# A partial sum put back into the accumulator banks, rounded channel sums, and a shift by matmul, in a one-core decoder step on Trainium2

## The chip, the cores and the metric

The kernel runs on one core of one Trainium2 chip. The metric is the device time of one execution in microseconds (us). A kernel's time is the median of several executions.

## What is computed

One step of a hybrid decoder with two layers, over 1024 prompt tokens and 8 sampled tokens, with 2048 channels. The first layer is a pooling mixer with a SiLU gate, the second a sliding-window attention with a gate. Around each layer stands a normalization with a scaled residual. Cut to the matrix products and what the change touches:

```python
# layer A
z = x @ w_in;  u, gate = z[..., :D_POOL], z[..., D_POOL:]          # "ai"
d = multiscale_pool(u) - u;  d = einsum(d, w_grp) * scale
h = layer_norm(ALPHA * x + (d * silu(gate)) @ w_out, g, b)         # "ao"
kv = h @ w_kv
# layer B
z = h @ w_in;  q, gate = z[..., :D_ATTN], z[..., D_ATTN:]          # "bi" (with kv)
o = attn_core(rope(q), k, v, window=128, sinks)
y = layer_norm(ALPHA * h + (o * silu(gate)) @ w_out, g, b)         # "bo"

def layer_norm(x, g, b):
    mu = mean(x);  var = mean(square(x - mu))
    return (x - mu) * rsqrt(var + LN_EPS) * g + b
```

Everything is held with the channels on the 128 partitions and the tokens along the free dimension, so a mean over channels is a sum over partitions and over 16 tiles.

## The kernel before, in words

**Phases and products.** The four big projections are the phases ai, ao, bi and bo, with 16, 8, 18 and 8 positions; a position is a pair of 128-channel output tiles (m = 0 and 1). The tokens are two chunks: c = 0 with 512, and c = 1 with 520 (512 prompt tokens and the 8 sampled ones). Each position is a 2x2 block product in seven multiplications, idx 0 to 6, instead of eight. A phase does them in three groups: A (idx 0 and 5, one unit of 512 columns each), C (idx 1, 3 and 6) and B (idx 2 and 4). Units of C and B have two halves of 260 columns (HV), and a half is a tick of 24 matmuls; a unit of A makes two ticks of 12 matmuls. In the last four positions of bo B all units of the first half come before those of the second.

**Passes.** Every operand is split into a rounded part and a rest, both in the four-byte matmul format fp32r: a ScalarE cast makes the first (L384 for weights, L515 for activations) and a VectorE subtraction the second (L392, L521). Each product is three fp32r matmuls, high by high, high by low and low by high: L588, L589 and L590 in `run_unit`.

**Banks.** A ring of three PSUM banks (`psD`) holds what is being accumulated, one bank is for small sums (`psO`), and four are for attention or for the tail (`psW`). `post` empties a bank after its tick:
- idx 0: the negated product is stored to DRAM (`n0`; L612).
- idx 1 and 3: group C starts from the negated product of idx 0, which `seed` loads nine ticks ahead and ScalarE copies into the bank at two ticks and one tick ahead (L677). The partial sums after idx 1 and idx 3 go to z[:, 0] and z[:, 1], by ScalarE (L625) in ai and bi, and by VectorE with the scaled residual (L621) in ao and bo. At idx 3 z is stored to DRAM (`bb`) through GpSimd's queue.
- idx 5 and 6: the outputs of the first chunk (L632).
- idx 2 starts a fresh bank, and idx 4 goes on in it. VectorE empties it after idx 2 as z[:, 1] less the bank (L641), which is the output m = 1 of the second chunk, and after idx 4 as the bank with z[:, 0] (L643 in ao and bo, L645 in ai and bi), which is m = 0. `recall` loads z nine ticks ahead (L698).
- For the gate channels of ai, a ScalarE Silu (L739) runs over each finished pair of tiles of the second chunk, eight in all.

**Normalization.** A side generator (`ln_gen`) normalizes a chunk, some steps per tick. Its sums over channels are in `j_gen`: for each stretch two fp32 matmuls of the constant J, which fills every partition with the mean (L813). L884 to L901 are its elementwise steps; L887 is the scale and bias on ScalarE. The output of the first position pair is used to shift all others ahead of squaring: its mean is made by fp32 matmuls in `shifted` (L1097) and, for the second chunk of bo, in `tail_full` (L1156). For bo B from position 2 on, the shift is subtracted on VectorE from both halves of z (L701). `tail_sums` (L1231), `tail_stats` (L1243 to L1245) and `tail_norm2` (L1261) end the kernel with the last outputs; L1193 and L1197 square and add the last pieces. What is left of the generators when the units are through is stepped before `tail_end`.

**Attention in bi.** Scores (L1429) go to the four banks `pS`, are copied (L1491) and masked on VectorE (L1492); L1293 applies the rotation to a tile whose partner was fetched by copies from SBUF to SBUF; L1572 is the activation of the gate.

**The order.** Instructions go to each engine in the order in which the program writes them (`in_order`). A planner writes them: `on` and `at` put an action at a tick with a rank; `soft` gives it to an engine with a due tick and lets it go early when that engine's metered work is less than 1.5 us ahead of TensorE's; the side generators step when VectorE and ScalarE are calm, or every few ticks, if four whole slots of the 53 SBUF slots are free. `start` loads the constants (cst, which holds J, at L1747) and makes the first operands.

Of the kernel before, what the change touches and what calls it, by code (L numbers as in the profile page):

```python
# [16 lines left out]
P = 128  # L17
# [139 lines left out]
class Kern:  # L157
    def __init__(self, ctx, tc, io):
# [17 lines left out]
        self.sgd = [one.tile([P, 8, NDEC], F32, name=f"sgd{i}") for i in range(2)]  # L176
        self.mem = Mem(pool("mem", bufs=1), NSLOT)
# [388 lines left out]
    def run_unit(self, u):  # L566
# [7 lines left out]
        for n, cs in enumerate(hs):  # L574
            w = cs.stop - cs.start
            key = ph, pos, cs.start
            if idx in (0, 2):
                self.bank[key] = self.psD()
            new = idx in (0, 2)
            ps = self.bank[key]  # L580
            for n2 in range(8):
# [12 lines left out]
                if u.grp == "A" and n2 == 3:  # L594
                    self.end()
            if n == len(hs) - 1:
                self.w_done(u)
# [3 lines left out]
    def post(self, u, cs):  # L601
# [13 lines left out]
        elif idx in (1, 3):  # L615
# [4 lines left out]
            if ph in RES:  # L620
                nc.vector.scalar_tensor_tensor(  # L621
                    z, z, ALPHA, ps[:, :w], op0=ALU.mult, op1=ALU.add if i else ALU.subtract
                )
            else:
                nc.scalar.copy(z, ps[:, :w])  # L625
            if idx == 3 and fin:
                nc.gpsimd.dma_start(self.bb[ph][:, pos], s.v(2, TMAX))
                self.bs.pop((ph, pos)).free(True)
# [7 lines left out]
        else:  # L636
            z = self.bs[ph, pos].v(2, TMAX)
            m = 1 if idx == 2 else 0
            out = self.dest(ph, pos, m, 1)(cs)
            if m:  # L640
                nc.vector.tensor_sub(out, z[:, 1, cs], ps[:, :w])  # L641
            elif ph in RES:
                nc.vector.tensor_add(out, ps[:, :w], z[:, 0, cs])  # L643
            else:
                nc.vector.tensor_sub(out, ps[:, :w], z[:, 0, cs])  # L645
            if m == 0:
# [6 lines left out]
    def prepare(self):  # L653

        for u in self.units:
# [4 lines left out]
            elif u.idx == 2 and u is self.firstu(u):  # L660
                self.recall(u)

    def firstu(self, u):
        return u if self.tick[u.ph, u.pos, u.idx] == u.t else None
# [26 lines left out]
    def recall(self, u):  # L691
        ph, pos, t = u.ph, u.pos, u.t
        nc = self.nc
        s = {}

        def load():
            b = self.bs[ph, pos] = self.mem.full()
            nc.sync.dma_start(b.v(2, TMAX), self.bb[ph][:, pos])  # L698
        def shift():
            z = self.bs[ph, pos].v(2, TMAX)  # L700
            nc.vector.tensor_sub(z, z, self.sh[:, None, :].to_broadcast([P, 2, TMAX]))  # L701

        self.on(t - 9, load, 5)
        if ph == "bo" and pos > 1:
            self.on(max(t - 7, self.first["bo", "B"] + 7), lambda: self.soft("v", self.i, t - 2, shift))
# [21 lines left out]
    def done(self, ph, pos, m, c, cs=None):  # L727
        k = ph, pos // 2, m, c
        if ph == "ai":
# [6 lines left out]
            elif i % 2:  # L736
                s = self.box.pop(k)
                if c == 1:
# [67 lines left out]
    def j_gen(self, T, src, out):  # L806

        J = self.cst[:, K_J : K_J + P]
        for s in [slice(0, T)] if T <= 512 else HV:
            yield from self.quiet()  # L810
            ps = self.psO()[:, : s.stop - s.start]
            for i, a in enumerate(src):
# [1155 lines left out]
```

## Time and profile before

| what | us |
|---|---|
| median of 3 executions | 2356.5 |
| lowest and highest | 2353.34, 2358.8 |
| the profiled execution | 2353.2 |
| its span | 2351.4 |
| mean granted TensorE clock, share of full | 0.991 |
| ScalarE's casts of weights L384, 366 | 380.2 |
| VectorE's subtractions L392, 366 | 444.7 |
| waits of TensorE on other engines, the sum of its table of waits | 33.1 |

The stages in the profiled execution, in us from the start of the span: ai A from 7.9, C from 211.5, B from 510.2; ao A from 741.6, C from 832.3, B from 970.3; bi A from 1065.9, C from 1313.4, B from 1667.9; bo A from 1955.6, C from 2073.3, B from 2211.6 to 2327.4; the tail to 2351.4.

In a row of waits "PE pD L588 <- DVE m L641: 10.9, 5, 6.1" TensorE (PE) waited at line 588 for VectorE (DVE) at line 641, 10.9 us in all, five times, 6.1 at the longest. In a row of groups stand the line, engine, operation, tiles and shape, the count, the busy time in us, the mean of one in ns, and the idle time of the engine just before them with what ended it. In a row of windows stand the stretch, its length, the busy time and number of instructions of PE, PE's weight loads, DVE, ACT (ScalarE) and POOL (GpSimd), the granted clock, the share of the DMA engines and GB/s. A row of the timeline has the start, the duration, the engine and the line; what stands in brackets is the idle time ahead of it. Matmul records of a row stand in the order of issue; an fp32 matmul leaves two records.

### The profile page before, as it was taken

What the parts mean: (1) busy time and instruction counts of PE and PEld (TensorE: products, weight loads), DVE (VectorE), ACT (ScalarE), POOL (GpSimd) and SP (SyncE); (2) the same over time, 40 slices, a digit from 0 to 9 for tenths busy, and PEclk for the clock granted to TensorE, in tenths of its full rate; (3) what the DMA queues carried; (4) which work ended last, traced back from release to release, by engine and by line L of the source; (5) the groups of instructions that cost most, each with busy time, mean ns of one, the idle gap of its engine ahead of it and who ended that gap; (6) DMA issues with size and microseconds to landing.
All of it is one profiled execution on the core that took longest, in us unless ns stands there. A gap on an engine that the chain in (4) does not pass through costs nothing. (4 is left out here: it accounts for less than half of the span.)

```text
span 2351.4 us, 41872 instructions
## 1 busy us (share of the span) xinstructions
PE 2297.0 (98%) x16998; PEld 2134.2 (91%) x16998; DVE 1550.3 (66%) x1884; ACT 1029.2 (44%) x2071; POOL 208.1 (9%) x424
## 2 busy tenths in 40 slices
PE   8999999999999999999999999999999999999985
PEld 6888999999999799998777899999999997899985
DVE  6456746656676686686765855665666777687686
ACT  4344333333233432444655635454646565542334
POOL 1101101000101111000110110100000000111002
PEclk9999999999999999999999999999999999999998
DMA  9858666674749798896685766666645566898843
GB/s 388 302 181 285 221 224 234 210 255 130 265 140 333 236 349 280 283 315 234 229 301 167 271 223 215 220 210 221 195 140 150 172 197 210 267 383 273 283 143 118
DMA packets 194481, 555.63 MB, mean 236 GB/s; under 512 B 31088, under 2 KB 36080, under 8 KB 194288
## 3 DMA queue, kind: packets, MB, share of 16 engines
q1 hardware_dynamic: 152592, 402.42, 52.9%
q0 software_dynamic: 41696, 150.55, 16.4%
q8 instruction: 133, 2.18, 0.4%
q14 instruction: 60, 0.49, 0.1%
HBM read 372.04 MB, written 171.33 MB: 231 GB/s over the span
## 5 line engine op out<-in xcount | busy, mean ns | idle before, releaser
L588 PE MATMUL pD<-m,m 128*128 128x260 f32 (+1 forms) x4800 | 1463.1, 305 | 19.0 <-DVE m L641 10.9
L589 PE MATMUL pD<-m,m 128*128 128x260 f32 (+1 forms) x4800 | 1448.4, 302 | 0.9 <-DVE m L521 0.9
L590 PE MATMUL pD<-m,m 128*128 128x260 f32 (+1 forms) x4800 | 1448.0, 302 | 0.0
L588 PEld LDWEIGHTS pD<-m,m 128*128 128x128 f32 x4800 | 906.1, 189 | 72.5 <-issue 26.2
L589 PEld LDWEIGHTS pD<-m,m 128*128 128x128 f32 x4800 | 906.5, 189 | 37.4 <-DVE m L521 2.0
L590 PEld LDWEIGHTS pD<-m,m 128*128 128x128 f32 x4800 | 905.9, 189 | 35.9
L392 DVE TENSOR_TENSOR m<-m,m 128x1024 fp32r<-128x1024 f32 x366 | 444.7, 1219 | 181.4 <-ACT m L384 167.1
L384 ACT CAST m<-m 128x1024 fp32r<-128x1024 f32 x366 | 380.2, 1045 | 77.6 <-PE pD L589 15.2
L428 DVE TENSOR_TENSOR m<-m,m 128x1024 f32<-128x1024 f32 x200 | 243.8, 1219 | 20.2 <-PE pD L589 6.5
L632 ACT COPY m<-pD 128x260 f32<-128x260 f32 (+1 forms) x126 | 55.9, 444 | 325.2 <-PE pD L590 319.2
L625 ACT COPY m<-pD 128x260 f32<-128x260 f32 x136 | 51.1, 376 | 225.8 <-PE pD L590 225.6
L521 DVE TENSOR_TENSOR m<-m,m 128x1040 fp32r<-128x1040 f32 x112 | 135.2, 1235 | 16.9 <-ACT m L515 16.6
L515 ACT CAST m<-m 128x1040 fp32r<-128x1040 f32 x112 | 114.7, 1059 | 37.4 <-DMA m<-h 17.8
L1492 DVE TENSOR_TENSOR m<-pS,cst 128x1024 f32<-128x1024 f32 x32 | 39.1, 1222 | 93.8 <-ACT m L1491 93.7
L1465 ACT ACTIVATE m<-m,sm 128x128 f32<-128x128 f32 x256 | 99.2, 391 | 0.0
L641 DVE TENSOR_TENSOR m<-m,pD 128x260 f32<-128x260 f32 x100 | 42.2, 422 | 75.3 <-PE pD L590 75.2
L1030 PE MATMUL pD<-m,m 128*128 128x260 f32 (+1 forms) x576 | 91.5, 319 | 0.0
L1030 PEld LDWEIGHTS pD<-m,m 128*128 128x128 f32 x576 | 82.0, 188 | 8.3
L1478 ACT ACTIVATE m<-m,sm 128x128 f32<-128x128 f32 x256 | 81.8, 393 | 7.2 <-DVE sm L1473 7.1
L612 ACT ACTIVATE m<-pD 128x512 f32<-128x512 f32 x50 | 29.8, 596 | 124.2 <-PE pD L590 114.8
L1446 ACT COPY m<-pS 128x768 f32<-128x768 f32 (+1 forms) x32 | 29.1, 908 | 123.0 <-PE pS L1429 123.0
L645 DVE TENSOR_TENSOR m<-pD,m 128x260 f32<-128x260 f32 x68 | 29.0, 426 | 73.1 <-PE pD L590 72.9
(168 smaller groups left out, 1564.1 us busy)
## 6 DMA issues: line engine op xcount, KB each, us to landing
m<-in_wia SPq DMA_DIRECT2D x96, 512.0 KB, 5.4
m<-in_wib SPq DMA_DIRECT2D x96, 512.0 KB, 5.0
m<-in_woa SPq DMA_DIRECT2D x48, 512.0 KB, 5.7
m<-in_wob SPq DMA_DIRECT2D x48, 512.0 KB, 6.8
m<-in_x SPq DMA_DIRECT2D x36, 520.0 KB, 9.8
sbi<-m POOLq DMA_DIRECT2D x36, 512.0 KB, 4.2
m<-sbi SPq DMA_DIRECT2D x36, 512.0 KB, 4.5
sai<-m POOLq DMA_DIRECT2D x32, 512.0 KB, 5.0
```

What stands on the lines that cost most here:

```text
L384: self.nc.scalar.copy(e["hi"].r[:, :1024], e["raw"].a[:, :1024])
L392: self.nc.vector.tensor_sub(o.r[:, :1024], s.a[:, :1024], e["hi"].a[:, :1024])
L428: self.nc.vector.tensor_add(s[o].a[:, :1024], s[a].a[:, :1024], s[b].a[:, :1024])
L515: self.nc.scalar.copy(h.r[:, : 2 * TMAX], s.a[:, : 2 * TMAX])
L521: self.nc.vector.tensor_sub(o.r[:, : 2 * TMAX], s.a[:, : 2 * TMAX], h.a[:, : 2 * TMAX])
L588: nc.tensor.matmul(ps[:, :w], wh[:, s], h, start=new and n2 == 0, stop=False, skip_group_check=on)
L589: nc.tensor.matmul(ps[:, :w], wh[:, s], l, start=False, stop=False, skip_group_check=on)
L590: nc.tensor.matmul(ps[:, :w], wl[:, s], h, start=False, stop=n2 == 7, skip_group_check=on)
L632: self.evac(ph, pos)(self.dest(ph, pos, m, 0)(cs), ps[:, : cs.stop - cs.start])
L1030: nc.tensor.matmul(ps[:, : cs.stop - cs.start], ws[:, s], d[:, cs], start=f0 and k == 0, stop=l0 and k == 3,)
L1465: nc.scalar.activation(x["s3"][:, i, :], x["s3"][:, i, :], AF.Exp, bias=nm[:, i : i + 1], scale=0.125, accum_out=rs[:, i : i + 1],)
L1478: nc.scalar.activation(x["s3"][:, i, :], x["s3"][:, i, :], AF.Copy, scale=rs[:, i : i + 1])
```

## The change

- The second-chunk banks of idx 2 start from the partial sum: `recall` lets ScalarE copy z[:, 1], now stored negated, into the bank, at two ticks and one tick before its half. After idx 2 the bank is emptied by a ScalarE activation with scale -1, which also applies the Silu for the gate channels of m = 1, so four of the eight Silus of L739 go. After idx 4 VectorE adds z[:, 0], which a new VectorE operation (`both`) has combined from z[:, 0] and z[:, 1] in group C, up to four ticks after idx 3; the store to `bb` follows it.
- The channel sums are made of rounded parts: VectorE adds the two tiles of the pair, ScalarE rounds the sum, VectorE takes the rest, and two fp32r matmuls of a rounded J (`jr`, copied on ScalarE in `start`) sum them. The shift's means round their input once (`rough`). `tail_sums` stays in fp32.
- The shift of bo B is applied in the bank by one fp32r matmul of `jr` per half-unit for positions above 1, 24 in all; `tail_full` makes its two right-hand sides (`shr`) on ScalarE and holds one slot more for them.

```diff
@@ -176,2 +176,3 @@
         self.sgd = [one.tile([P, 8, NDEC], F32, name=f"sgd{i}") for i in range(2)]
+        self.jr = one.tile([P, P], F32R, name="jr")[:]
         self.mem = Mem(pool("mem", bufs=1), NSLOT)
@@ -576,5 +577,5 @@
             key = ph, pos, cs.start
-            if idx in (0, 2):
+            new = idx == 0
+            if new:
                 self.bank[key] = self.psD()
-            new = idx in (0, 2)
             ps = self.bank[key]
@@ -595,2 +596,4 @@
                     self.end()
+            if (ph, u.grp) == ("bo", "B") and pos > 1:
+                nc.tensor.matmul(ps[:, :w], self.jr, self.shr[idx][:, cs], start=False, stop=True, skip_group_check=True)
             if n == len(hs) - 1:
@@ -621,4 +624,6 @@
                 nc.vector.scalar_tensor_tensor(
-                    z, z, ALPHA, ps[:, :w], op0=ALU.mult, op1=ALU.add if i else ALU.subtract
+                    z, z, -ALPHA if i else ALPHA, ps[:, :w], op0=ALU.mult, op1=ALU.subtract
                 )
+            elif i:
+                nc.scalar.mul(z, ps[:, :w], -1.0)
             else:
@@ -626,4 +631,16 @@
             if idx == 3 and fin:
-                nc.gpsimd.dma_start(self.bb[ph][:, pos], s.v(2, TMAX))
-                self.bs.pop((ph, pos)).free(True)
+
+                def both():
+                    z = s.v(2, TMAX)
+                    if ph in RES:
+                        nc.vector.tensor_sub(z[:, 0], z[:, 0], z[:, 1])
+                    else:
+                        nc.vector.scalar_tensor_tensor(
+                            z[:, 0], z[:, 1], -1.0, z[:, 0], op0=ALU.mult, op1=ALU.subtract
+                        )
+                    nc.gpsimd.dma_start(self.bb[ph][:, pos], z)
+                    s.free(True)
+
+                self.bs.pop((ph, pos))
+                self.soft("v", self.i, self.i + 4, both)
         elif idx in (5, 6):
@@ -636,3 +653,2 @@
         else:
-            z = self.bs[ph, pos].v(2, TMAX)
             m = 1 if idx == 2 else 0
@@ -640,8 +656,6 @@
             if m:
-                nc.vector.tensor_sub(out, z[:, 1, cs], ps[:, :w])
-            elif ph in RES:
-                nc.vector.tensor_add(out, ps[:, :w], z[:, 0, cs])
+                f = AF.Silu if ph == "ai" and pos % 8 > 3 else AF.Copy
+                nc.scalar.activation(out, ps[:, :w], f, scale=-1.0)
             else:
-                nc.vector.tensor_sub(out, ps[:, :w], z[:, 0, cs])
-            if m == 0:
+                nc.vector.tensor_add(out, ps[:, :w], self.bs[ph, pos].v(2, TMAX)[:, 0, cs])
                 del self.bank[key]
@@ -659,8 +673,5 @@
                 self.seed(u)
-            elif u.idx == 2 and u is self.firstu(u):
+            elif u.idx == 2:
                 self.recall(u)
 
-    def firstu(self, u):
-        return u if self.tick[u.ph, u.pos, u.idx] == u.t else None
-
     def seed(self, u):
@@ -692,4 +703,2 @@
         ph, pos, t = u.ph, u.pos, u.t
-        nc = self.nc
-        s = {}
 
@@ -697,10 +706,12 @@
             b = self.bs[ph, pos] = self.mem.full()
-            nc.sync.dma_start(b.v(2, TMAX), self.bb[ph][:, pos])
-        def shift():
-            z = self.bs[ph, pos].v(2, TMAX)
-            nc.vector.tensor_sub(z, z, self.sh[:, None, :].to_broadcast([P, 2, TMAX]))
+            self.nc.sync.dma_start(b.v(2, TMAX), self.bb[ph][:, pos])
 
-        self.on(t - 9, load, 5)
-        if ph == "bo" and pos > 1:
-            self.on(max(t - 7, self.first["bo", "B"] + 7), lambda: self.soft("v", self.i, t - 2, shift))
+        def put(cs):
+            ps = self.bank[ph, pos, cs.start] = self.psD()
+            self.nc.scalar.copy(ps[:, :THM], self.bs[ph, pos].v(2, TMAX)[:, 1, cs])
+
+        if u.hs[0] is HV[0]:
+            self.on(t - 9, load, 5)
+        for n, cs in enumerate(u.hs):
+            self.on(t - 2 + n, lambda cs=cs: put(cs), 0)
 
@@ -737,3 +748,3 @@
                 s = self.box.pop(k)
-                if c == 1:
+                if c == 1 and m == 0:
                     self.nc.scalar.activation(s.a[:, : 2 * TMAX], s.a[:, : 2 * TMAX], AF.Silu)
@@ -805,12 +816,23 @@
 
-    def j_gen(self, T, src, out):
+    def j_gen(self, T, s, out):
 
-        J = self.cst[:, K_J : K_J + P]
-        for s in [slice(0, T)] if T <= 512 else HV:
+        nc = self.nc
+        v = self.pair_view(s, T)
+        nc.vector.tensor_add(v[:, 0], v[:, 0], v[:, 1])
+        yield
+        w = self.mem.full()
+        hi, lo = w.r[:, :T], w.r[:, TMAX : TMAX + T]
+        nc.scalar.copy(hi, v[:, 0])
+        yield
+        nc.vector.tensor_sub(lo, v[:, 0], hi.bitcast(F32))
+        s.free()
+        yield
+        for h in [slice(0, T)] if T <= 512 else HV:
             yield from self.quiet()
-            ps = self.psO()[:, : s.stop - s.start]
-            for i, a in enumerate(src):
-                self.nc.tensor.matmul(ps, J, a[:, s], start=i == 0, stop=i == len(src) - 1)
-            out(s, ps)
+            ps = self.psO()[:, : h.stop - h.start]
+            for i, a in enumerate((hi, lo)):
+                nc.tensor.matmul(ps, self.jr, a[:, h], start=i == 0, stop=i == 1)
+            out(h, ps)
             yield
+        w.free()
 
@@ -845,3 +867,2 @@
         flat = lambda s: s.a[:, : 2 * T]
-        a2 = self.pair_view(acc, T)
         load(0)
@@ -849,4 +870,3 @@
         load(1)
-        yield from self.j_gen(T, [a2[:, 0], a2[:, 1]], lambda s, ps: nc.scalar.copy(mu[:, s], ps))
-        acc.free()
+        yield from self.j_gen(T, acc, lambda s, ps: nc.scalar.copy(mu[:, s], ps))
         w = self.mem.full()
@@ -870,5 +890,4 @@
                 yield
-        s2 = self.pair_view(sq, T)
         yield from self.j_gen(
-            T, [s2[:, 0], s2[:, 1]],
+            T, sq,
             lambda s, ps: nc.vector.scalar_tensor_tensor(v[:, s], ps, EPS, q[:, s], op0=ALU.add, op1=ALU.subtract)
@@ -876,3 +895,2 @@
         )
-        sq.free()
         self.rstd(v, rr, q)
@@ -1091,9 +1109,13 @@
 
+        def rough():
+            box["r"] = self.mem.full()
+            nc.scalar.copy(box["r"].r[:, : 2 * T], flat(s))
+
         def mean():
-            t = self.pair_view(s, T)
             ps = self.psO()
-            J = self.cst[:, K_J : K_J + P]
+            t = box["r"].rv(2, T)
             for j in range(2):
-                nc.tensor.matmul(ps[:, :T], J, t[:, j], start=j == 0, stop=j == 1)
+                nc.tensor.matmul(ps[:, :T], self.jr, t[:, j], start=j == 0, stop=j == 1)
             nc.scalar.mul(self.l_sh.a[:, :T], ps[:, :T], NK / 2.0)
+            box.pop("r").free()
 
@@ -1121,2 +1143,3 @@
             pre[0] = s
+            self.at(0, rough)
             self.product(1, mean, 1)
@@ -1135,2 +1158,4 @@
         self.sh = self.shs.a
+        two = self.mem.full()
+        self.shr = {2: two.r[:, :TMAX], 4: two.r[:, TMAX:]}
         self.tp, self.tq, self.L, self.R = {}, {}, {}, {}
@@ -1151,3 +1176,8 @@
 
+        def rough():
+            self.trough = self.mem.full()
+            nc.scalar.copy(self.trough.r[:, : 2 * TMAX], flat(s))
+
         def mean():
+            t = self.trough.rv(2, TMAX)
             for h in HV:
@@ -1155,4 +1185,7 @@
                 for j in range(2):
-                    nc.tensor.matmul(ps, J, self.tv(q)[:, j, h], start=j == 0, stop=j == 1)
-                nc.scalar.mul(self.sh[:, h], ps, NK / 2.0)
+                    nc.tensor.matmul(ps, self.jr, t[:, j, h], start=j == 0, stop=j == 1)
+                nc.scalar.mul(self.shr[2][:, h], ps, 8.0 * NK)
+            self.trough.free()
+            nc.scalar.mul(self.sh, self.shr[2].bitcast(F32), 1.0 / 16)
+            nc.scalar.mul(self.shr[4], self.shr[2].bitcast(F32), -2.0)
 
@@ -1174,2 +1207,3 @@
         if q == 4:
+            self.at(0, rough)
             self.product(1, mean, 1)
@@ -1752,2 +1786,3 @@
         es[1]["low"]()
+        nc.scalar.copy(self.jr, self.cst[:, K_J : K_J + P])
         nc.vector.tensor_scalar(
```

## The prediction, as it was written ahead of the result

> **What bounds the kernel now.** I read the page first, then PE's waits, then busy time by stage.
>
> ```profile
> span 2351.4 us, 41872 instructions
> PE 2297.0 (98%) x16998; PEld 2134.2 (91%) x16998; DVE 1550.3 (66%) x1884; ACT 1029.2 (44%) x2071; POOL 208.1 (9%) x424
> PE pD L588 <- DVE m L641: 10.9, 5, 6.1
> PE pS L1429 <- DVE m L1492: 10.6, 4, 4.6
> 741.60:832.30 90.70, 90.70 (x390) 72.83 (x390) 57.01 (x53) 34.82 (x43) 11.45 (x26) 1.00 0.83 284
> 832.30:970.30 138.00, 138.00 (x1153) 138.00 (x1152) 97.34 (x106) 48.43 (x70) 13.69 (x24) 1.00 0.87 309
> ```
>
> TensorE is the bound: it is busy 98% of the span, and its two largest waits are 10.9 us (five times, on L641, the VectorE emptying of the second-chunk banks) and 10.6 us (four times, on the attention mask L1492). The two rows by stage are ao A and ao C. A time can fall in three ways only: fewer or cheaper matmul passes, fewer waits of TensorE, or a shorter head or tail. They also price a matmul: ao C holds 8 positions x 6 half-units x 24 = 1152 matmuls of 260 columns in 138.0 us, 0.120 us each (a tick of 24 is 2.88); ao A holds 384 of 512 columns and one channel sum of 1.7 us, 0.232 each. VectorE is busy 97 of 138 us in ao C, ScalarE 48: the room on ScalarE is the larger.
>
> **The change part by part.**
>
> *Channel sums.* The fp32 matmuls of J become fp32r ones.
>
> ```profile
> L813 PE MATMUL pO<-m,cst 128*128 128x512 f32 x16 | 7.5, 592 | 0.0
> L813 PE MATMUL pO<-m,cst 128*128 128x260 f32 x16 | 4.2, 383 | 0.0
> L1097 PE MATMUL pO<-m,cst 128*128 128x512 f32 x8 | 3.9, 605 | 0.6 <-DVE m L1521 0.6
> L1156 PE MATMUL pD<-m,cst 128*128 128x260 f32 x8 | 1.9, 382 | 0.0
> 766.35 0.40 PE L590 MATMUL pD<-m,m 128*128 128x512 f32 x1
> 766.59 1.88 PE L1097 MATMUL pO<-m,cst 128*128 128x512 f32 x4
> 767.90 0.79 PE L588 MATMUL pD<-m,m 128*128 128x512 f32 x1
> 2233.51 1.91 PE L1156 MATMUL pD<-m,cst 128*128 128x260 f32 x8
> 2235.26 1.88 PE L813 MATMUL pO<-m,cst 128*128 128x512 f32 x4
> ```
>
> An fp32 matmul leaves two records. A pair of 512 columns is four: between the ends of the neighbours (766.75 and 768.69) lie 1.94 us, less the neighbour's own 0.23, so 1.71. Eight records of 260 take 1.75 (2233.51 to 2235.26). There are 24 records of 512 (6 pairs) and 24 of 260 (3 sets): 6 x 1.71 + 3 x 1.75 = 15.5 us. After: 12 fp32r matmuls of 512 and 12 of 260, at the prices above 12 x 0.232 + 12 x 0.120 = 4.2. **-11.3.** The Trainium skill ("FP8 and Floating Point Precision", TensorE Precision Notes) says that true FP32 makes four passes; by four passes of those prices the sums would be 16.9 and the gain an estimated 12.7; the rows show 3.7 passes' time, and the measurement decides. The added VectorE add, ScalarE cast and VectorE subtraction come before each sum; they lengthen the chain of a normalization, which is spread over tens of ticks, and cost nothing but in the tail.
>
> *Shift by matmul.* 24 matmuls of 260 columns more: 24 x 0.120 = **+2.9**.
>
> *Emptying and filling.*
>
> ```profile
> L641 DVE TENSOR_TENSOR m<-m,pD 128x260 f32<-128x260 f32 x100 | 42.2, 422 | 75.3 <-PE pD L590 75.2
> L625 ACT COPY m<-pD 128x260 f32<-128x260 f32 x136 | 51.1, 376 | 225.8 <-PE pD L590 225.6
> L677 ACT COPY pD<-m 128x260 f32<-128x260 f32 x100 | 38.5, 386 | 0.0
> L739 ACT ACTIVATE m<-m 128x1040 f32<-128x1040 f32 x8 | 8.6, 1075 | 45.9 <-DVE m L641 33.9 <-DVE m L645 12.0
> L771 DVE TENSOR_TENSOR m<-m,m 128x520 f32<-128x520 f32 (+1 forms) x32 | 22.1, 691 | 0.0
> ```
>
> 100 emptyings of 0.42 leave VectorE; ScalarE gets 100 of 0.38 and 100 fills of 0.39, less four Silus of 1.08: 72 us more on an engine that is busy 44%. VectorE gets 50 combinations of 520 columns at 0.69 (35 us) in the C stages. All lie beside TensorE as long as a fill is done before its bank's first matmul and an emptying before the ring of three comes round. What no row shows is a fill from ScalarE in a B stage. Bounds: below, the 100 fills of L677 in the C stages never appear among PE's waits, so 0, and less than 0 it cannot be, since a fill shortens nothing. Above: the bank of idx 2 is used again by idx 4 two ticks after, so its emptying has one tick, 2.88, of which it needs 0.38: 2.5 us of slack. A pair of casts ahead of it in the queue (2.02, below) does not use that up; an activation that stands waiting 4.11 us for VectorE, as L1572 does below, would make it 1.6 late, 80 us if at each of 50 positions. I take 0, nearest to L677, which has the same form, the same due time two ticks ahead and the same ring. The recalled tile is loaded nine ticks (26 us) ahead; the fill needs it seven (20 us) ahead, and the slowest copies below landed in 11. The store of that tile now follows the combination, up to four ticks later, on GpSimd's queue; its reader is a group away. In bi A the order of ScalarE's instructions holds two more switches of its function table; nothing waits for ScalarE there in PE's waits, so nothing.
>
> *Waits that go.* First bo B:
>
> ```profile
> 2281.50:2287.60 6.10, 0.03 (x2) 0.04 (x1) 6.07 (x7) 0.77 (x2) 0.00 (x0) 0.81 0.41 160
> 2287.60:2292.60 5.00, 5.00 (x25) 5.00 (x26) 1.40 (x3) 0.64 (x1) 0.00 (x0) 0.55 0.00 0
> PE pD L588 <- DVE m L641: 9.9, 4, 6.1
> 2322.70 0.51 PE L588 MATMUL pD<-m,m 128*128 128x260 f32 x1 [2.16 <-DVE m L641]
> L701 DVE TENSOR_TENSOR m<-m,m 128x1040 f32<-128x1040 f32 x6 | 7.4, 1233 | 0.0
> 2318.05 0.63 ACT L1193 ACTIVATE m<-m 128x520 f32<-128x520 f32 x1
> ```
>
> The third row is the waits of 2211 to 2328. The group is of VectorE from 2240 to 2289: six shifts, 7.4 us of its work ahead of the emptyings there. VectorE is busy in 6.07 of the first row's 6.10 us, the emptying stands at the end of its queue, TensorE waits 6.07 us for it and then runs at 0.55 of its clock: 25 matmuls in 5.0 instead of 3.0. ScalarE is busy 0.77 of those 6.10 us. With the shift gone and the emptying there, 6.07 + 2.0 and a small wait of 0.7 go: **-8.8.** After such a wait the Trainium skill ("TensorE: Matmul & The Clock Gate", Part 1) has the clock halved by an idle window of about 3.4 us; the 0.55 agrees. The last two waits (9.9 - 6.07 - 0.7 = 3.1 us, 2.16 of it at 2322.70) I leave: there ScalarE has normalization pieces such as L1193 ahead. The fifth wait of L641 (10.9 - 9.9 = 1.0, in ai B) loses **-0.7**. Next bi:
>
> ```profile
> 1808.30 1.07 ACT L1572 ACTIVATE m<-m 128x1040 f32<-128x1040 f32 x1 [4.11 <-DVE m L641]
> 1809.28 0.99 ACT L1491 COPY m<-pS 128x1024 f32<-128x1024 f32 x1
> 1810.31 1.23 DVE L1492 TENSOR_TENSOR m<-pS,cst 128x1024 f32<-128x1024 f32 x1 [2.04 <-ACT m L1491]
> 1183.50:1192.00 8.50, 3.93 (x18) 2.54 (x16) 8.26 (x9) 0.00 (x0) 0.52 (x2) 0.66 0.90 362
> 1190.00:1195.00 5.00, 5.00 (x23) 3.58 (x20) 3.85 (x6) 1.75 (x2) 1.08 (x2) 0.70 0.63 220
> L1293 DVE TENSOR_TENSOR m<-m,m 128x1024 f32<-128x1024 f32 x2 | 2.4, 1222 | 6.5 <-DMA m<-m 6.5
> m<-m SPq DMA_DIRECT2D x4, 128.0 KB, 11.0
> ```
>
> Three of the four waits on L1492 (10.6 - 4.6 = 6.0) are this pattern of bi B: L1572 waits for the VectorE emptying, L1491 stands behind it and L1492 behind that. With the emptying on ScalarE itself each loses about half: **-3.0**. The fourth, 4.57 us in bi A, comes from VectorE, where L1293 waited 6.5 us for rope copies that landed in 11.0 with the DMA engines full (0.90). With the slow clock behind it (3.93 us of PE at 0.66 and 3.0 more at 0.70: 2.2) it costs 6.8. The change adds generator steps and puts the first normalization of B, whose traffic this is, five to six ticks later, behind those copies: **-6.8**, the least sure term; above, it is 0.
>
> *Head and tail.*
>
> ```profile
> 16.10 1.05 ACT L384 CAST m<-m 128x1024 fp32r<-128x1024 f32 x1 [2.94 <-DMA m<-in_wia]
> 17.05 2.02 ACT L515 CAST m<-m 128x1040 fp32r<-128x1040 f32 x2
> 10.81 0.34 SPq L1747 DMA_DIRECT2D cst<-in_cst  x1
> cst<-in_cst SPq DMA_DIRECT2D x1, 222.0 KB, 8.9
> 2327.85 1.50 ACT L887 ACTIVATE m<-m,prm 128x512 f32<-128x512 f32 x2
> 2329.57 2.07 ACT L1261 ACTIVATE m<-m,prm 128x260 f32<-128x260 f32 x4
> 2331.55 0.35 ACT L1243 COPY m<-pD 128x260 f32<-128x260 f32 x1
> ```
>
> The rounded J is copied on ScalarE as soon as cst is there, 10.81 + 8.9 = 19.7, and stands ahead of casts that ran at 16.10 and 17.05 and feed the third unit. The first of them moves to 19.9, 3.8 us later. How much of that the third unit feels hangs on how far ahead the casts ran, which no row shows; between 0 and 3.8 I take the middle, **+2.0**. In the tail the later generator leaves three pairs of L887's normalization to run between the last emptying and L1243, six of 0.71 (a pair is 1.50): **+4.3** (0 if VectorE's chain hides them).
>
> Sum: -11.3 + 2.9 - 8.8 - 0.7 - 3.0 - 6.8 + 2.0 + 4.3 = **-21.4**. Against the profiled run's 2353.2 (span 2351.4 and 1.8 around it) that is 2331.8. That run lies 3.3 under the median of 2356.5, so on the median's scale 2335.1: I predict **2335**.
>
> **Rivals.**
> (a) The bi A stall stays, or one like it comes elsewhere, since DMA engines are 0.83 to 0.87 busy in the ao stages too: 2335 + 6.8 = **2342**. For it: nothing in the change touches the copies themselves.
> (b) bo B's stall stays as a wait behind ScalarE work that itself waits for VectorE (L1193 waits for VectorE's subtractions): 2335 + 8.8 = **2344**. Against it: ScalarE is nearly empty in the stall.
> (c) Slower: ScalarE's queue. VectorE's emptying stood behind arithmetic only; ScalarE's stands behind activations that wait for VectorE, as L1572 did for 4.11 us. Where one does, the emptying is 4.11 - 2.5 = 1.6 us late and TensorE with it. The gain of 21.4 is gone when that happens at 13 of the 50 positions; at half of them it costs 25 x 1.6 = 40: 2335 + 40 = **2375**. Against it: ao C, with fills and emptyings by ScalarE, is busy 138.00 of 138.00. The Trainium skill ("PSUM — Partial Sum Buffer", Engine vs sequencer instructions) calls ScalarE's queue strict FIFO; the L1491 that ran only behind L1572 at 1809.28 agrees.
> (d) The change doesn't do what it says: the fp32r sums cost as before, 2335 + 11.3 = **2346**. Against it: L588 to L590 are fp32r and cost 0.120.
>
> **How the numbers follow.** Forecast, 2322 to 2340: 0.52 (low end without the start and tail terms and with the last waits gone: 2335 - 6.3 - 3.1 = 2325.7, less one small wait more). (a) 0.17, (b) 0.07, (d) 0.04. Half of (c), about as before: 0.08. (c): 0.12. The range takes in (a), (b), (d) and part of the half of (c): 2322 to 2356. A measurement tells apart about 0.2%, 4.7 us: faster (under 2351.8) 0.80, same 0.08, slower 0.12.
>
> **What would show it.** Right: in PE's waits L641 vanishes; no ScalarE fill or emptying (new L711, L658) with more than 3 us in all; J's records are 24, with 0.23 and 0.12 between them; bo B is about 107 us instead of 115.8; VectorE has 57 us less minus 35 in the C stages; the first normalization of bi runs behind the rope copies. Wrong: PE waiting for L711 in many places, a clock under 0.99, a C stage that is longer (the combinations late), or a wait on a recall.

## The result

The changed kernel takes 2350.39 us, the kernel before 2354.04 (medians of 20 executions each); the ratio is 0.9984, 95% interval 0.9977 to 0.9991. It is faster by 3.7 us, clear of the noise of 20 executions but inside the 0.2% that the prediction called no change. Forecast were 21.4 us. The profiled execution took 2350.32 us, with a span of 2348.5 and a clock of 0.990: 2.9 us less than the profiled execution before. That is what has to be explained: 18.5 us of the forecast are missing. A trace shows a single execution, and the 20 executions of the kernel after lie up to 6.4 us apart, those of the kernel before up to 9.3; which waits repeat in other traces is said where they matter.

The page of the kernel after (its lines are shifted: the passes are L589 to L591, the fill is L711, the new emptying L658, the mask L1526, the casts L385 and L516):

```profile
span 2348.5 us, 42019 instructions
PE 2290.5 (98%) x16998; PEld 2132.3 (91%) x16998; DVE 1547.3 (66%) x1840; ACT 1100.6 (47%) x2281; POOL 208.6 (9%) x424
```

VectorE's busy time hardly falls and ScalarE's rises by 71 us, as forecast (72). TensorE's busy time falls by 6.5. PE's waits after:

```profile
PE pS L1463 <- DVE m L1526: 8.8, 4, 3.9
PE pD L589 <- ACT m L516: 7.9, 1, 7.9
PE pD L589 <- ACT pD L711: 7.8, 3, 5.1
PE pD L589 <- ACT m L658: 1.2, 1, 1.2
```

The 10.9 us on VectorE's emptying are gone. In their place stand 7.8 us on the new fill (5.1 and 0.5 in ao B, 2.2 in bo B) and 1.2 on the new emptying (in bo B), and the mask still costs 8.8. Then the stages, by the starts of their first matmuls. First the kernel before, then the kernel after, each with ao B, bi A, bi B, and bo B with the tail:

```profile
970.30:1065.90 95.60, 95.60 (x778) 93.68 (x777) 77.04 (x89) 41.91 (x48) 5.30 (x13) 1.00 0.87 295
1065.90:1313.40 247.50, 240.84 (x1239) 191.70 (x1239) 161.73 (x185) 130.85 (x283) 28.19 (x68) 0.99 0.72 244
1667.90:1955.60 287.70, 281.19 (x2532) 267.44 (x2530) 200.96 (x302) 157.81 (x446) 11.54 (x20) 1.00 0.54 166
2211.60:2351.40 139.80, 109.25 (x818) 104.85 (x816) 105.25 (x133) 56.38 (x86) 13.05 (x9) 0.90 0.44 147
```

```profile
970.40:1072.00 101.60, 95.98 (x775) 95.38 (x774) 72.10 (x76) 53.13 (x81) 5.38 (x13) 0.97 0.82 274
1072.00:1313.90 241.90, 237.63 (x1231) 190.03 (x1230) 165.39 (x190) 134.52 (x287) 28.24 (x68) 0.99 0.74 253
1668.30:1957.60 289.30, 283.11 (x2532) 268.51 (x2530) 188.61 (x267) 181.78 (x519) 11.57 (x20) 0.99 0.53 167
2212.70:2348.50 135.80, 104.66 (x833) 102.11 (x832) 96.19 (x115) 69.72 (x122) 13.04 (x9) 0.91 0.44 152
```

The first number behind the stretch is its length. ao B became 6.0 us longer, though its channel sums got cheaper: TensorE, which never waited there, now does (95.98 busy of 101.60). bi A became 5.6 shorter, bi B 1.6 longer, bo B with the tail 4.0 shorter; the stages ahead of ao B end 0.1 later than before, the start's 2.0 included.

**ao B.** The timeline of ScalarE and of TensorE around the wait:

```profile
1045.11 1.06 ACT L516 CAST m<-m 128x1040 fp32r<-128x1040 f32 x1 [5.73 <-DMA m<-h]
1046.48 1.06 ACT L516 CAST m<-m 128x1040 fp32r<-128x1040 f32 x1 [0.31 <-DMA m<-h]
1047.45 1.51 ACT L905 ACTIVATE m<-m,prm 128x512 f32<-128x512 f32 x2
1048.87 0.36 ACT L711 COPY pD<-m 128x260 f32<-128x260 f32 x1
```

```profile
1049.29 0.59 PE L589 MATMUL pD<-m,m 128*128 128x260 f32 x1 [5.09 <-ACT pD L711]
```

The cast of bi A's first operands waits 5.73 us for the load of h, which ao B's normalization has only just made. Two casts and a pair of normalizations later the fill runs, and TensorE had waited 5.09 us for it. With the slow clock behind it (0.50 from 1049.3 to 1054.7), the half-units there come 7.7 us later. The kernel before has such waits too, in the same stretch:

```profile
1047.92 1.06 ACT L515 CAST m<-m 128x1040 fp32r<-128x1040 f32 x1 [2.85 <-DMA m<-h]
1055.79 1.06 ACT L515 CAST m<-m 128x1040 fp32r<-128x1040 f32 x1 [5.40 <-DMA m<-h]
```

They cost nothing there, because nothing that TensorE needed soon stood behind them. The wait repeats: in the four other traces with these fills and sums in ao B (the copy of J later, the pause, the pace and the leftovers, below) it is 5.5 to 6.1 us.

**bo B.** A second fill is late there, and an emptying at the half-unit behind it. The normalization's activation waits for VectorE, and the fill stands behind it:

```profile
2303.12 1.10 ACT L1295 ACTIVATE m<-m,prm 128x260 f32<-128x260 f32 x2 [5.35 <-DVE m L1287]
2305.54 0.37 ACT L711 COPY pD<-m 128x260 f32<-128x260 f32 x1
```

```profile
2305.95 0.39 PE L589 MATMUL pD<-m,m 128*128 128x260 f32 x1 [2.16 <-ACT pD L711]
```

By the starts of the half-units this fill costs 2.4 us and the emptying 0.3, and the 2.2 us that the kernel before waits for VectorE's last emptying there are gone, so that it nearly cancels.

**bi A.** The stall of 1183 to 1192 went (6.7 us by the starts of the half-units), and one like it came 55 us later (6.6 us), at the next set of rope copies. VectorE, TensorE and the copies after:

```profile
1238.78 2.36 DVE L1327 TENSOR_TENSOR m<-m,m 128x1024 f32<-128x1024 f32 x2 [5.11 <-DMA m<-m]
```

```profile
1243.59 3.79 PE L1463 MATMUL pS<-m,m 64*128 64x256 f32 x16 [3.85 <-DVE m L1526]
```

```profile
m<-m SPq DMA_DIRECT2D x4, 128.0 KB, 11.4
```

The copies land in 11.4 us, as the earlier set did before (11.0). In their turn, the earlier set of 1170 lands in 6.2 after. This wait too repeats at the same place, with 2.7 to 4.7 us, in the three other traces that have the same code in bi A.

### The profile page after: what moved, and what is told of

Same layout as the page of the kernel before. It is cut to its first block, busy times and chain, and to the rows that moved or that the text cites. A ratio compares the mean times of both kernels' runs of the same rounds, so it can differ in the third digit from the quotient of the medians.

```text
span 2348.5 us, 42019 instructions
## 1 busy us (share of the span) xinstructions
PE 2290.5 (98%) x16998; PEld 2132.3 (91%) x16998; DVE 1547.3 (66%) x1840; ACT 1100.6 (47%) x2281; POOL 208.6 (9%) x424
## 5 line engine op out<-in xcount | busy, mean ns | idle before, releaser
L589 PE MATMUL pD<-m,m 128*128 128x260 f32 (+1 forms) x4800 | 1459.7, 304 | 17.8 <-ACT m L516 7.9
L591 PE MATMUL pD<-m,m 128*128 128x260 f32 (+1 forms) x4800 | 1447.9, 302 | 0.0
L589 PEld LDWEIGHTS pD<-m,m 128*128 128x128 f32 x4800 | 905.8, 189 | 70.7 <-issue 15.6
L591 PEld LDWEIGHTS pD<-m,m 128*128 128x128 f32 x4800 | 905.7, 189 | 35.9
L393 DVE TENSOR_TENSOR m<-m,m 128x1024 fp32r<-128x1024 f32 x366 | 445.0, 1219 | 185.5 <-ACT m L385 169.3
L385 ACT CAST m<-m 128x1024 fp32r<-128x1024 f32 x366 | 381.0, 1045 | 48.8 <-PE pD L590 13.4
L429 DVE TENSOR_TENSOR m<-m,m 128x1024 f32<-128x1024 f32 x200 | 243.8, 1219 | 19.6 <-PE pD L590 7.1
L658 ACT ACTIVATE m<-pD 128x260 f32<-128x260 f32 x100 | 38.6, 386 | 202.2 <-PE pD L591 183.2
L516 ACT CAST m<-m 128x1040 fp32r<-128x1040 f32 x112 | 114.5, 1059 | 19.6 <-DVE m L393 6.5
L1526 DVE TENSOR_TENSOR m<-pS,cst 128x1024 f32<-128x1024 f32 x32 | 39.2, 1224 | 120.2 <-ACT m L1525 120.2
L660 DVE TENSOR_TENSOR m<-pD,m 128x260 f32<-128x260 f32 x100 | 42.6, 426 | 113.8 <-PE pD L591 106.4
L628 ACT ACTIVATE m<-pD 128x260 f32<-128x260 f32 x68 | 26.4, 388 | 117.1 <-PE pD L591 117.0
L630 ACT COPY m<-pD 128x260 f32<-128x260 f32 x68 | 25.6, 376 | 110.5 <-PE pD L591 110.5
```

Source lines behind the costliest of these rows:

```text
L385: self.nc.scalar.copy(e["hi"].r[:, :1024], e["raw"].a[:, :1024])
L393: self.nc.vector.tensor_sub(o.r[:, :1024], s.a[:, :1024], e["hi"].a[:, :1024])
L429: self.nc.vector.tensor_add(s[o].a[:, :1024], s[a].a[:, :1024], s[b].a[:, :1024])
L516: self.nc.scalar.copy(h.r[:, : 2 * TMAX], s.a[:, : 2 * TMAX])
L589: nc.tensor.matmul(ps[:, :w], wh[:, s], h, start=new and n2 == 0, stop=False, skip_group_check=on)
L591: nc.tensor.matmul(ps[:, :w], wl[:, s], h, start=False, stop=n2 == 7, skip_group_check=on)
```

## The experiments

Theory: the forecast's gains were there, and two waits that it didn't have gave them back: in ao B a fill behind a cast that waits for a transfer, in bi A the old stall at the next copies. Rival: the later normalization alone makes both. For each experiment stand its median time and its ratio to the kernel before, timed beside it, with the 95% interval. That is mostly some 2 us to either side, so experiments that differ by less are not told apart by their times.

### The rounded sums alone

The kernel before with `jr`, the new `j_gen`, `rough` and the copy in `start`; fills, emptying and shift as before.

> The kernel before with the rounded channel sums alone (and the copy of J in the start); emptying, filling and shift as before. Theory (the forecast gains are there, and new waits give them back: in ao B a fill by ScalarE behind a cast that waits for a DMA, 7.8 us; in bi A the old stall on the partner copies, only 55 us later, 6.6 us): no wait above 2 us in ao B, the bi A stall of about 6.6 at 1250 instead of 1188, the 6 us wait of bo B kept, start +2, tail +4 to 6: 2354.0 - 11.3 + 2 + 5 = about 2350. Rival (the ao B stall comes from the later normalization and so from the sums): a wait of 5 us or more in ao B here too, about 2357.

Measured: 2352.62 us, ratio 0.9992 (0.9983 to 1.0001). ao B takes 92.8 us and TensorE waits for nothing there. The bi A stall sits at the later place (5.6 us of waiting and the slow clock). Against the expectation the 6 us wait of bo B has gone as well, though VectorE still empties and shifts: VectorE's timeline has none of the normalization's subtractions from 2255 to 2275, where the kernel before has several; they come later. And all that bo B gained, and more, is lost in the tail, as the stretch from bo B to the end and ScalarE's timeline in it show:

```profile
2205.80:2348.40 142.60, 103.08 (x811) 100.75 (x809) 108.16 (x137) 58.79 (x89) 12.58 (x9) 0.87 0.43 144
```

```profile
2314.67 4.38 ACT L895 ACTIVATE m<-m,prm 128x512 f32<-128x512 f32 x6
2319.86 1.52 ACT L895 ACTIVATE m<-m,prm 128x512 f32<-128x512 f32 x2 [0.82 <-DVE m L909]
2322.32 1.52 ACT L895 ACTIVATE m<-m,prm 128x512 f32<-128x512 f32 x2 [0.94 <-DVE m L909]
2324.65 1.52 ACT L895 ACTIVATE m<-m,prm 128x512 f32<-128x512 f32 x2 [0.82 <-DVE m L909]
2327.11 1.52 ACT L895 ACTIVATE m<-m,prm 128x512 f32<-128x512 f32 x2 [0.94 <-DVE m L909]
2328.53 0.35 ACT L1263 COPY m<-pD 128x260 f32<-128x260 f32 x1
```

142.6 us instead of 139.8. L895 is the scale and bias of the first chunk: seven leftover pairs run from 2314.67 to 2328.53 ahead of L1263, which opens the last chain.

### Fills, emptying and shift alone

The kernel after with the fp32 `j_gen`, `shifted` and mean of `tail_full`.

> The kernel after with the fp32 channel sums of before; fills and emptyings by ScalarE and the shift by matmul stay. Theory: the ao B wait on the fill (5 us and a slow clock behind it, 7.8) is there, the bi A stall is back at about 1188, bo B is 6 to 9 us shorter: 2354.0 + 2 (start) + 2.9 (shift) - 8.8 (bo B) - 3.7 (ai B, bi B) + 7.8 (ao B) = about 2354. Rival (the later normalization makes the ao B stall): no wait above 2 us in ao B, about 2346.

Measured: 2348.65 us, 0.9982 (0.9973 to 0.9991): half of the change does as well as the whole. ao B takes 95.7 us with no wait. My theory's number failed, and the first run had already failed the rival's: neither half makes the ao B wait. It needs both. Nor is the stall of bi A back at 1188, as I expected: it is gone here too (6.6 us by the half-units' starts), and at the next set of copies TensorE waits for the mask only 1.7 us.

### The fills of ao B by VectorE

```diff
-            self.nc.scalar.copy(ps[:, :THM], self.bs[ph, pos].v(2, TMAX)[:, 1, cs])
+            z = self.bs[ph, pos].v(2, TMAX)[:, 1, cs]
+            if ph == "ao":
+                self.nc.vector.tensor_copy(ps[:, :THM], z)
+            else:
+                self.nc.scalar.copy(ps[:, :THM], z)
```

> The kernel after with the fills of ao B made by VectorE instead of ScalarE, all else as it is. Theory (the fill stands in ScalarE's queue behind a cast that waits for a DMA): the 5.1 us wait at about 1046 and its slow clock go, ao B is 7.8 us shorter and the whole about 2342.6, unless the later stages shift. Rival (the banks or VectorE's own queue are late there): a wait of 3 us or more stays in ao B, 2348 to 2351.

Measured: 2349.30 us, 0.9977 (0.9968 to 0.9986); ao B 99.4 us.

```profile
PE pD L589 <- DVE pD L713: 5.1, 3, 2.3
```

The wait at 1049 is gone, as the theory had it: that one is ScalarE's queue. But three shorter waits stand earlier in ao B, because the fill is late in VectorE's queue too; by the time, the rival is nearer. The timeline of VectorE ahead of the longest of them:

```profile
1017.90 1.23 DVE L923 TENSOR_TENSOR m<-m,m 128x1024 f32<-128x1024 f32 x1
1019.04 0.42 DVE L660 TENSOR_TENSOR m<-pD,m 128x260 f32<-128x260 f32 x1
1019.38 0.42 DVE L713 COPY pD<-m 128x260 f32<-128x260 f32 x1
```

VectorE works without a gap from 1012.3 to 1028.8, and what stands ahead of the fill is the normalization's subtraction and multiplication (L922, L923), a subtraction of weights (L393) and an emptying (L660), none of them waiting for a transfer.

### The copy of J later

```diff
-        nc.scalar.copy(self.jr, self.cst[:, K_J : K_J + P])
+        self.on(40, lambda: nc.scalar.copy(self.jr, self.cst[:, K_J : K_J + P]))
```

> The kernel after with the copy of the rounded J made 40 ticks into the kernel instead of in the start. Theory (the copy waits for its load ahead of the casts of the third unit): the third unit starts 2.0 us earlier, at 21.4 instead of 23.4, and all of ai with it: about 2348.4. Rival (the lead is lost again at the next load): the third unit is earlier but ai A ends at 213.3 as in the kernel after, 2350.4.

Measured: 2348.65 us, 0.9978 (0.9969 to 0.9987). The third unit starts at 21.5 us, and ai C at 211.4 instead of 213.3. Of the 2.0 us, 1.6 are left in the span (2346.9). The medians alone would not tell this run from the kernel after; the starts do.

### One generator step in place of three

The two yields between add, cast and subtraction in `j_gen` taken out.

> The kernel after with one generator step in place of three ahead of each channel sum (the add, the cast and the subtraction are made in one step). Theory (the ao B wait needs both the fills on ScalarE and the normalization made later by these steps, as neither the sums alone nor the fills alone showed it; the pairs left for the tail come from the same steps): the 5 us wait in ao B goes (7.7 us with its slow clock), the stretch from the last half-unit's start to the end falls from 35.0 to 31 to 32: about 2340. Rival (what is late is the step's own chain, not the number of steps): ao B stays at 101.6 us or TensorE waits for the sums themselves, 2348 to 2352.

Measured: 2350.07 us, 0.9983 (0.9975 to 0.9992). ao B falls to 95.2 us and its wait to 1.0, and the stretch from the last half-unit's start to the end to 32.0: that half held. But bi A rises from 241.9 to 250.7: both sets of copies now stall it (7.5 us of waits on the mask). What ao B gave, bi A took. The time is the rival's, but not for the rival's reason.

### A pause of the generators behind the copies

```diff
             box["t"] = self.partner(s, n, T)
+            if not c:
+                self.stepped = self.i + 4
```

> The kernel after in which the side generators pause for four ticks more behind each set of partner copies of the first chunk in bi A. Theory (the copies land late because the normalization's and the t-tiles' traffic fills the DMA engines): the copies of the third set land in 5 to 7 us instead of 11.4 and the 3.9 us wait on the mask at 1243 with its slow clock goes, 6.6 us: about 2343.8, unless the pause makes the tiles late for bi C. Rival (the copies are slow by themselves or by the weights' traffic): they land in 10 us or more and the wait stays, 2350.

Measured: 2369.71 us, 1.0072 (1.0059 to 1.0084): slower. The copies of the third set (issued from 1226 on) land in 7.5 us, the wait at 1243 goes, and by the half-units' starts 6.6 us with it. This supports the generators' traffic as the cause of that stall; the pause holds their work on VectorE and ScalarE back too, but what VectorE waited for there was the copies. But the traffic has to pass ahead of bi C: its first operands and the last copies come late.

```profile
PE pS L1465 <- DVE m L1528: 11.8, 1, 11.8
PE pD L589 <- ACT m L516: 9.3, 1, 9.3
```

The two waits end at 1307.5 and 1333.9; they are three times what was saved.

### A step at every tick in bo B

`pace(2)` to `pace(1)` at the start of bo B.

> The kernel after with the side generator allowed a step at every tick in bo B instead of every second. Theory (the steps come too seldom, so pairs are left over for the tail, while VectorE is idle for 15 of the last 56 us of bo B): no pair is left behind the last emptying, the stretch from the last half-unit's start to the end falls from 35.0 to about 30, 2346. Rival (VectorE is the bound of bo B): waits on its emptying come back in bo B, and the end stays where it is, 2349 to 2351.

Measured: 2351.24 us, 0.9993 (0.9984 to 1.0001). VectorE has no pair left behind its last emptying, and the span is the same 2348.4: the pieces now stand among the last emptyings and squares, the last half-unit starts 3.9 us later, and TensorE waits 2.6 us on L658 one half-unit ahead of it and, behind it, 2.2 on L1231, a VectorE addition of squares. The rival's view held.

### Four edits together

The copy of J later, one step, the pause and the pace.

> The kernel after with four edits: the copy of the rounded J later, one step in place of three, the pause in bi A and the faster pace in bo B. Theory: the gains add up, 2350.4 - 2 - 7.7 - 6.6 - 4 = about 2330. Rival (each edit shifts the meeting of transfers and queues in bi A, and a stall of the same size comes back at another place): 2336 to 2343.

Measured: 2353.76 us, 1.0000 (0.9991 to 1.0009). The sum was far off, and so was the rival's 2336 to 2343: bi A and bi C have two waits of 6.1 and 6.3 us where one of 3.9 had been.

### Only the means of the shift rounded

Fills alone, with `rough` in `shifted` and `tail_full` and the copy of J later.

> Fills, emptyings and shift as in the kernel after, the channel sums of the normalizations in fp32 as before, the two means of the shift rounded (no generator step is added by them), and the copy of the rounded J 40 ticks into the kernel. Theory (the parts that add no steps keep their gains): the 2348.65 of fills alone less 2.0 (start), 0.7 (the mean in ao A) and 1.3 (the mean in bo B): about 2344.6. Rival (every shift of the start changes how the transfers meet in bi A): the stages up to bi A are 4 us earlier, but bi C starts no earlier than in fills alone, 2348 to 2350.

Measured: 2350.13 us, 0.9982 (0.9973 to 0.9991). In the trace ao A starts 1.8 us earlier than in fills alone; bi C starts 8.3 later (1319.0 against 1310.7), as a wait of 6.0 us is back at 1192 in bi A. This trace is of an execution 3.5 us above the run's median, so 8.3 is more than the usual loss. By the ratios the two runs are alike: none of the 4 us that were expected is there, and so far the rival held.

### The sums by one rounding

```diff
-        nc.vector.tensor_add(v[:, 0], v[:, 0], v[:, 1])
-        yield
         w = self.mem.full()
-        hi, lo = w.r[:, :T], w.r[:, TMAX : TMAX + T]
-        nc.scalar.copy(hi, v[:, 0])
-        yield
-        nc.vector.tensor_sub(lo, v[:, 0], hi.bitcast(F32))
+        nc.scalar.copy(w.r[:, : 2 * T], s.a[:, : 2 * T])
         s.free()
         yield
```

The matmuls then take the two rounded tiles.

> As the run before it in this list, and the channel sums of the normalizations by one ScalarE rounding of the pair and two fp32r matmuls, without the rest part: one more generator step per sum instead of three, and no VectorE work (the sums lose the rest part's digits). Theory (three steps per sum are what made the normalizations late): no wait above 2 us in ao B, and 6 pairs and sets of the old sums' 9 become cheaper, 11.3 - 2.0 = 9.3 us less: about 2336. Rival (TensorE's gain in ao B and bi A is taken back by the transfers there): bi C starts no earlier than 1309, about 2343.

Measured: 2346.77 us, 0.9968 (0.9955 to 0.9980), the lowest median of all, 7.9 us under the kernel before (of five executions, and the interval overlaps those of several others). ao B takes 94.8 us with 0.8 of waits on ScalarE; bi A takes back 6 us of waits on the mask, and bi C starts at 1310.8, as the rival said; 2336 was far off, and the time lies above the rival's 2343 as well.

### Empty steps and no rounded sums

Fills alone, with the fp32 sums and three empty yields ahead of each.

> Fills alone (fp32 channel sums), with three empty generator steps ahead of each channel sum and no other work. Theory (the ao B wait comes from the lateness of the normalization together with the fill behind the cast, not from the sums' added instructions): a wait of about 5 us on the fill in ao B, which takes about 102 us instead of 95.7: 2354 or more. Rival (the added VectorE and ScalarE instructions make it): no wait above 2 us in ao B, 2349.

Measured: 2357.94 us, 1.0014 (1.0005 to 1.0023). The wait is back without one added instruction; PE's waits from 970 to 1072, and the stage:

```profile
PE pD L589 <- ACT pD L711: 5.3, 2, 4.8
PE pD L589 <- ACT m L658: 1.6, 1, 1.6
```

```profile
971.00:1077.00 106.00, 99.06 (x779) 96.52 (x778) 69.77 (x72) 51.92 (x79) 5.31 (x13) 0.97 0.79 267
```

The long wait comes as in the kernel after, with the cast that waits for h ahead of the fill in ScalarE's queue:

```profile
1049.17 1.06 ACT L516 CAST m<-m 128x1040 fp32r<-128x1040 f32 x1 [4.86 <-DMA m<-h]
1053.54 0.36 ACT L711 COPY pD<-m 128x260 f32<-128x260 f32 x1
```

ao B takes 106.0 us against 95.7 without the empty steps. So what makes the ao B wait is that the normalization, and with it the load of h, comes a few ticks later, while a fill stands behind the cast that waits for it.

### The leftovers between the last normalizations

The leftover generator steps made inside `tail_end`, one after each normalization, instead of ahead of it.

> The kernel after with the leftover generator steps made between the last normalizations instead of ahead of them. Theory (six leftover activations stand ahead of the copy that opens the last chain, which has its data at 2322): that copy starts at about 2323 instead of 2328.4, and the end comes 2 to 3.5 us earlier, 2347 to 2348.4. Rival (VectorE's total work sets the tail): the copy is earlier and the end is not, 2350.

Measured: 2351.44 us, 0.9984 (0.9975 to 0.9993).

```profile
2321.88 0.35 ACT L1277 COPY m<-pD 128x260 f32<-128x260 f32 x1
2339.34 5.04 ACT L1295 ACTIVATE m<-m,prm 128x260 f32<-128x260 f32 x10
```

In the kernel after the copy runs at 2328.40 and the last L1295 end at 2344.7. Here the copy runs 6.5 us earlier (2.3 of it from earlier stages) and the last end at 2344.4: the leftover pairs lie in between and fill the time. The rival held: here the work of the tail set the end, not its order.

## Why the prediction was wrong, point by point

- **Channel sums, -11.3: right.** In the run with the sums alone the half-units behind the sums come earlier by 0.7 us in ao A, 2.6 in ao B, 2.6 in bi A, 1.2 in bo A and about 4 in bo B, some 11 in all.
- **Start, +2.0: right**, by the run with the copy later, though with luck: it was the middle of a range from 0 to 3.8. After, the copy runs at 19.68 and the cast behind it at 19.89 instead of 16.10.
- **ai B, -0.7**: 1.05, right. **bo B, -8.8**: 8.1, right in size. The reason was too narrow: each half of the change alone removes that wait, the sums by moving the normalization's pieces. **Tail, +4.3**: the three leftover pairs came as worked out. From the last half-unit's start to the end it is 28.7 us before and 35.0 after, so +6.3. The term was too small by 2.0 and knew only the generator: in fills alone, without the sums' steps and with one pair left, the stretch is already 32.0. So about 3.2 come with the fills and the shift and 3.1 with the steps, which in the sums alone leave seven pairs.
- **Shift, +2.9: right.** 24 matmuls as counted; a half-unit of bo B that waits for nothing takes 2.99 to 3.00 us after and 2.88 before.
- **bi B, -3.0: wrong in sign.** Two of the three waits lost 1.0 us each, as argued. The third I had misread: before, the activation waits for no emptying there, but stands behind a cast of weights that waits for VectorE's L1400. Before, and after:

```profile
1944.49 1.05 ACT L384 CAST m<-m 128x1024 fp32r<-128x1024 f32 x1 [1.73 <-DVE m L1400]
1945.45 1.07 ACT L1572 ACTIVATE m<-m 128x1040 f32<-128x1040 f32 x1
```

```profile
1944.42 1.05 ACT L385 CAST m<-m 128x1024 fp32r<-128x1024 f32 x1 [1.24 <-DVE m L1434]
1945.37 0.38 ACT L658 ACTIVATE m<-pD 128x260 f32<-128x260 f32 x1
1945.79 1.07 ACT L1606 ACTIVATE m<-m 128x1040 f32<-128x1040 f32 x1
1946.76 0.99 ACT L1525 COPY m<-pS 128x1024 f32<-128x1024 f32 x1
1949.07 3.68 PE L1463 MATMUL pS<-m,m 64*128 64x256 f32 x16 [3.23 <-DVE m L1526]
```

  The cast still waits, and the new emptying now stands in the queue ahead of the activation and the copy. The wait is 3.23 us instead of 2.27, and the 16 matmuls behind it run at 0.53 of the clock instead of 1.00 and take 3.68 us instead of 2.00; another wait of 0.8 at 1706 is new, and bi B is 1.6 us longer. How much of it the emptying makes was not taken apart: in the sums alone, where VectorE empties, this wait is 2.80 us, and in the sums by one rounding, with the new emptying but a cast that does not wait, 1.90.
- **bi A, -6.8: failed as rival (a) had it.** The stall moved to the next copies. The step that failed was to count the traffic in front of one set of copies only. The pause spoke for the traffic as the cause, and showed that putting it off by four ticks costs more than it saves. The reason given for the gain, that the added steps move the traffic behind the copies, does not hold either: in fills alone, without these steps, the old stall goes as well, and in the run with only the means rounded, also without them, it is back with 6.0 us (one trace each). What decides at which copies it comes stays open.
- **Fills at 0: the step that failed most.** It cost 7.7 us in ao B, in one place. I had a bound for a fill or an emptying held by an instruction that waits for VectorE, and gave rival (c) that mechanism at many positions. Just that mechanism, with a wait for VectorE, came at one position of bo B (2.4 us, which nearly cancels with the last emptying). What cost most is the same mechanism at one position of ao B, with the wait for a transfer in place of one for VectorE, and it needed the change's other half. That the time comes out about as before, where half of rival (c) was put, is luck: its price was for many positions. The row that shows it was in the profile before: casts that wait up to 5.40 us for h, with no price because nothing urgent stood behind them. I took group C's fills as the nearest row, but in ao C no such cast is in the queue.

One gain came that was not forecast. The kernel before has this among its waits:

```profile
PE pS L1483 <- ACT m L1478: 1.7, 1, 1.7
```

It stood at 1149 in bi A and is gone there; the half-units from 1153 on come 2.5 us earlier. The runs with three steps per sum all show that (the sums alone, the empty steps), fills alone doesn't. Which step moves it was not looked into.

The sum: forecast -21.4; ao B +7.7, bi A's stall +6.7, bi B +4.6 and tail +2.0 more than forecast, bo B +0.7 and ai B -0.3, the wait at 1149 -2.5: -2.5, against the measured -2.9. Left out are the changes at the end of bo B that nearly cancel (+2.4, +0.3, -2.2) and shifts of under 0.8 us each.

## What to carry to other kernels

Before moving work that TensorE needs at once to another engine, list what already waits in that engine's queue, transfers above all, even where that wait costs nothing today: moved work inherits it. Price every added step of a generator as a delay of everything the generator feeds, loads and leftovers in the tail among them. And where a stall comes from transfers that fill the DMA engines, a gain ahead of it is only a shift of the traffic; count the stall as kept until a run shows it gone.

## What was not expected of the hardware

The same 128 KB copies from SBUF to SBUF land in 2.3 us (median of the set at 1114, fills alone) and in 12.0 us (the set at 1219, sums alone), with different traffic around them: the DMA engines' share is 0.56 from 1112 to 1122 in the one and full (1.02) from 1218 to 1234 in the other. The share alone does not give the time: the set of 1170 in the kernel after lands in 6.2 us at 0.96 (1170 to 1182). And two edits without a wait can make one together: each half of this change leaves ao B without, and both give one of 5.1 us.
